# A hybrid attention and Fourier encoder layer: two operand splits issued later, and the middle frequency's column in one product with the first group's columns

## The chip, the cores and the metric

The kernel runs on one core of one Trainium2 chip. The metric is the device time of one execution in microseconds; the median of the runs counts. One execution was taken with the hardware profiler; its rows give start times in microseconds from the start of its span.

## The reference

One encoder layer is applied to a prompt of 256 tokens and, apart from it, to a sample of 2048 tokens, both 1024 wide, in float32.

```python
def encoder_layer(x, w_in, rpb, w_fourier, b_fourier, g_pre, g_na, g_f, w_out, g_post):
    h = rms_norm(x, g_pre)
    proj = h @ w_in
    q, k, v, z_a, u_f, z_f = jnp.split(proj, ...)
    y_a = neighbourhood_attention(q, k, v, rpb)
    y_f = fourier_mix(u_f, w_fourier, b_fourier)
    mixed = jnp.concatenate([rms_norm(y_a, g_na) * jax.nn.silu(z_a),
                             rms_norm(y_f, g_f) * jax.nn.silu(z_f)], axis=-1)
    out = mixed @ w_out
    return x + rms_norm(out, g_post)

def fourier_mix(u, w_f, b_f):
    ...
    spec = jnp.fft.fft2(ug, axes=(1, 3), norm='ortho')
    mixed = spec.real.reshape(b, s, F_WIDTH).astype(u.dtype)
    return mixed @ w_f + b_f
```

Six projections of 512 columns each leave the normed input. The attention looks at a window of 8 by 16 positions of a grid 64 wide. The Fourier part takes the real part of a transform over the tokens and over 64 columns of each of 8 groups.

## The kernel before, in words

**Precise products.** A float32 operand is split into a high half, a cast to a shorter form (ScalarE, ACT), and a low half, the remainder that the cast leaves (VectorE, DVE). A product is then three matmuls on TensorE (PE): high by high (L171), high by low (L172 or L173) and low by high. `mm3` issues them in this order. So each operand needs its cast, and then its remainder, ahead of the matmul that reads it. Products that are not split (the Fourier stage's `dft`, L1005) run in plain float32, and the trace shows each such product as two PE rows.

**The stages.** The trace has, in order: products for the prompt (weights folded with the norm's gains, the first tokens); 16 blocks of the prompt's other projections (`for b in range(16)`, PE rows `mm<-ph,wl` and the like, up to 121.5 us), whose weight blocks are split by `b_raw` (L577 cast `wh`, L578 remainder `wl`) two blocks ahead; the stage `vu(0)`, from 121.5 us on, which makes the sample's first half of the `v` and `u` projections; the sample's other projections; the Fourier stage (`stage2`, from 553 us on); attention and the output.

**vu(0) and its operands.** `vu` makes two outputs with seven products in place of eight: sums of blocks of the input times sums of blocks of the weights. There are 14 groups of 12 matmuls (seven products j = 0 to 6, two column strips s each, in the order 0 0 1 1 2 2 3 3 4 4 5 5 6 6). A group i at place j reads

- the operand `bnew[0, j]`, that is the high half `xh` and the remainder `xl` of a 128 by 2048 block of the sample, made by `n_first(j)`: the cast at L444 on ACT, the subtraction at L445 on DVE. Sums of such blocks come from `n_sum` (L439). `xl` is first read by the third matmul of its group (L173);
- the weight `op_[j]`, `vh` and `vl`, two halves each, made by `op_split` (L493 and L494, for j = 5 L489 and L490); `op_split(0)` and `op_split(1)` stand in blocks 14 and 15, the others in vu(0) at i = 2, 4, 6, 8 and 10. The weights from j = 2 on are loaded by `op_load` (L479) from a scratch tensor.

Each group's result leaves PSUM with a copy (L524 on ACT) or an addition (L521 on DVE: `uc`, `u`, `vuo`), and `vuo` is stored by SyncE (L364).

What else is done in vu(0) comes from a table of hooks, by the group index i: `n_first`, `rows_load` (L300, 1 MB of rows `xm`), `rows_square` (L305, two squares on ACT that add up a row's squares), `w_load`, `w_sums` (L548 on POOL, GpSimd) and `a_split` (L562, L563) of the next stage's weights. Row block x + 5 is loaded at i = 2x + 1 and squared at i = 2x + 4 for x = 0 to 3. The operands `xh`, `xl`, the blocks `nx` and the rows `xm` share one pool of 16 buffers of a megabyte each (tag `k8`).

Before the change `n_first` stands at block 3 (j = 0), 5 (j = 1), 12 (j = 2), 13 (j = 3) and in vu(0) at i = 0, 3 and 6 (j = 4, 5, 6). The engines work through their instructions in order. The order on each is close to the program's, but a tool places the instructions, so that it isn't word for word that of the code.

**stage2.** The Fourier transform over the tokens has two steps; `stage2(gq, zg, c)` is the second one, for four quarters gq and five column pieces c. For each pair it makes the 256 columns of a PSUM tile `pab` in four products of 64 columns (c = 4: four of three parts each), one per group g, with the matrices `d2`. `split_ab` then takes a high half (`split_ps`, L997; on DVE if gq = 0 and c < 3, else on ACT; L1012 for c = 4) and a remainder (L998, L1014) of them. For gq = 0 there is one more column, the middle frequency: a product of one column with `dnyq`, in a PSUM tile of its own, `pny` (tag `a`, three buffers), and its own `split_ab`. `pab` takes turns through three buffers: `b`, `b`, `c`, so that the fourth product reuses the first's, the fifth the second's and so on. Just before, DVE clears two PSUM tiles `ptb` (L975).

`dnyq` (128 by 4) holds the one-column matrix in column 0, zeros in 1 and a mask of partitions in column 2, which `pq` reads (L1055). It is loaded once, long before (L917).

Of the kernel before, what the change touches and what calls it, by code (L numbers as in the profile page):

```python
# [10 lines left out]
F32 = mybir.dt.float32  # L11
# [34 lines left out]
def constants():  # L46
    c = {}
    c["ident"] = np.eye(128, dtype=np.float32)
    n1 = np.arange(128)
    f1 = np.zeros((128, 128))  # L50
    for k1 in range(64):
        f1[:, 2 * k1] = np.cos(2 * np.pi * ((k1 * n1) % 128) / 128)
        f1[:, 2 * k1 + 1] = np.sin(2 * np.pi * ((k1 * n1) % 128) / 128) if k1 else (-1.0) ** n1
    c["f1"] = f1.reshape(32, 4, 128).transpose(1, 0, 2).reshape(128, 128)
    nrm = 1.0 / np.sqrt(2048 * 64)
    n2 = np.arange(16)
    d = np.zeros((128, 16, 128))
    for g in range(16):
        for kl in range(4):
            k1 = 4 * g + kl  # L60
            for k2 in range(16):
                if k1:
                    k = k1 + 128 * k2
                elif k2 < 8:
                    k = 128 * k2
                else:
                    k = 64 + 128 * (k2 - 8)
                co = np.cos(2 * np.pi * ((n2 * k) % 2048) / 2048) * nrm
                si = np.sin(2 * np.pi * ((n2 * k) % 2048) / 2048) * nrm
                ca = k2 * 4 + kl  # L70
                cb = 64 + ca
                r0 = (kl * 2) * 16 + n2
                r1 = (kl * 2 + 1) * 16 + n2
                if k1:
                    d[r0, g, ca] = co
                    d[r1, g, ca] = -si
                    d[r0, g, cb] = si
                    d[r1, g, cb] = co
                else:
                    r = r0 if k2 < 8 else r1  # L80
                    d[r, g, ca] = co
                    d[r, g, cb] = si
    c["d2"] = d
    dn = np.zeros((128, 4))
    dn[:16, 0] = ((-1.0) ** n2) * nrm
    dn[:, 2] = np.arange(128) % 32 != 0
    c["dnyq"] = dn
    n = np.arange(256)[:, None]
    k = np.arange(129)[None, :]
    ang = 2 * np.pi * ((n * k) % 256) / 256  # L90
    f256 = np.concatenate([np.cos(ang), np.sin(ang)], axis=1) / np.sqrt(256 * 64)
    c["f256"] = f256.reshape(4, 2, 32, 258).transpose(0, 2, 1, 3).reshape(128, 2, 258)
    f = np.arange(64)
    sl = np.arange(32)
    cs = np.zeros((128, 2, 64))
    for b in range(2):
        rows, cols = slice(64 * b, 64 * b + 64), slice(32 * b, 32 * b + 32)
        ang = 2 * np.pi * ((f[:, None] * sl[None, :]) % 64) / 64
        cs[rows, 0, cols] = np.cos(ang)
        cs[rows, 1, cols] = np.where(sl == 0, (-1.0) ** f[:, None], np.sin(ang))  # L100
    c["cs"] = cs
    cm = np.zeros((128, 2, 32))
    cs_ = np.zeros((128, 80))
    rm = np.zeros((128, 16))
    for p in range(128):
        half, i, qc = p // 64, p // 16 % 4, p % 16
        for b in range(2):
            cb = 2 * b + half
            ws = min(max(16 * cb + qc - 8, 0), 48)
            kc = KP0[cb] + np.arange(32)  # L110
            cm[p, b] = np.where((kc >= ws) & (kc < ws + 16), 0.0, BIG)
        for cb, j in ((0, slice(0, 24)), (1, slice(24, 56)), (3, slice(56, 80))):
            ws = min(max(16 * cb + qc - 8, 0), 48)
            kc = KC0[cb] + np.arange(KW[cb])
            cs_[p, j] = np.where((kc >= ws) & (kc < ws + 16), 0.0, BIG)
        j = np.array(ORD[half])
        rm[p, :11] = np.where((j >= i) & (j < i + 8), 0.0, BIG)
    c["cmask"] = cm.reshape(128, 64)
    c["csmask"] = cs_
    c["rmask"] = rm  # L120
    return {k: np.ascontiguousarray(v.astype(np.float32)) for k, v in c.items()}
# [54 lines left out]
def build(tc, A, O):  # L176
# [3 lines left out]
    cst = es.enter_context(tc.tile_pool(name="cst", bufs=1))  # L180
# [27 lines left out]
    invt = cst.tile([128, 18], F32, name="invt")  # L208
    invf = cst.tile([128, 18], F32, name="invf")
    inva = cst.tile([128, 18], F32, name="inva")  # L210
    dnyq = cst.tile([128, 4], F32, name="dnyq")
    cm = cst.tile([128, 80], F32, name="cm")[:, :64].rearrange("p (b x) -> p b x", b=2)


# [528 lines left out]
    for b in range(16):  # L743
        kind, blk = divmod(b, 4)
        if b < 10:
            wz_load(1)
        if b in (0, 2):
            n_load((b // 2, 1))
        if b == 10:
            op_load(0)  # L750
        if b == 12:
            op_load(1)
        if b < 14:
            b_raw(b + 2)
        if b < 8:
            x, y = divmod(b, 2)
            n_scale(None, *divmod(x, 2)[::-1], range(2 * y, 2 * y + 2))
        elif b < 12:
            n_sum(b - 8)
        if b in (3, 5, 12, 13):  # L760
            n_first((3, 5, 12, 13).index(b))
        if b > 13:
            op_split(b - 14)
        p = mmt(512)[:, :TP]
        wh, wl = wb.pop(b)
        for k in range(KC):
            mm3(nc, p, wh[:, k], wl[:, k], hp_[:, k], lp_[:, k], k == 0, k == KC - 1)
        o = st.tile([128, 256], F32, tag="f", name="f", bufs=3)
        if kind == 1:
            v = [(o, p)]  # L770
        elif kind == 3:
            v = [(o[:, 128 * x:128 * x + 128].rearrange("p (x r c) -> p r x c", x=2, c=16),
                  p[:, 128 * x:128 * x + 128].rearrange("p (r x c) -> p r x c", x=2, c=16)) for x in range(2)]
        else:
            v = [(o.rearrange("p (r b c) -> p b r c", b=2, c=32), p.rearrange("p (b r c) -> p b r c", b=2, c=32))]
        for d, i in v:
            nc.scalar.activation(d, i, AF.Silu if kind < 2 else AF.Copy, scale=-0.125 if kind == 3 else 1.0)
        if kind < 2:
            nc.sync.dma_start(zD[kind, blk * 128:blk * 128 + 128, :TP], o)
        else:  # L780
            nc.sync.dma_start((kD if kind == 2 else qD)[blk, :, :TP], o)
# [14 lines left out]
    def at(i, f, *a):  # L796
        hooks.setdefault(i, []).append(call(f, *a))

    for x in range(4, 7):
        at(3 * x - 12, n_first, x)  # L800
    for x in range(4):
        at(2 * x + 1, rows_load, x + 5)
        at(2 * x + 4, rows_square, x + 5)
# [212 lines left out]
    def stage2(gq, zg, c):  # L1016
        m = int(c in (2, 3))
        np_ = 96 if c == 4 else 128
        x = (gq * 5 + c) % 3 == 2
        p = ps.tile([np_, 4, 64], F32, tag="c" if x else "b", name="pab", bufs=1 if x else 2)  # L1020
        for g in range(4):
            dft(p[:, g, :], c, [(zg[g], d2[gq // 2][:, (gq % 2) * 4 + g, m * 64:m * 64 + 64])])
        split_ab(gq, c, lambda a: a[:, :1024].rearrange("p (k q g l) -> p q g k l", k=16, q=4, g=4)[:, gq],
                 p.rearrange("p g (k l) -> p g k l", l=4))
        if gq == 0:
            p = ps.tile([np_, 1], F32, tag="a", name="pny")
            dft(p, c, [(zg[0], dnyq[:, m:m + 1])])
            split_ab(gq, c, lambda a: a[:, 1024:1025], p)
        if gq == 2:
            p = ps.tile([np_, 129], F32, tag="a", name="pup")  # L1030
            dft(p, c, [(up[:, t], f256[:, t, 129 * m:129 * m + 129]) for t in range(2)])
            split_ab(gq, c, lambda a: a[:, 1025:1154], p)
# [6 lines left out]
    def pq(m):  # L1039
        PQ[m] = [gt([128, 2, 512], F32R, "pq" + x) for x in "hl"]  # L1040
        pp = [ps.tile([128, 512], F32, tag="a", name="ppq") for b in range(2)]
        for j in range(4):
            for b in range(2):
                rs = slice(64 * b, 64 * b + 64)
                nc.tensor.matmul(pp[b][32 * j:32 * j + 32], cs2[rs, m, 32 * b:32 * b + 32], wf[rs, j, :], start=True,
                                 stop=True)
        for b, p in enumerate(pp):
            h, l = PQ[m][0][:, b], PQ[m][1][:, b]
            if m == 0:
                split_ps(h, l, p)  # L1050
                continue
            t = sm.tile([128, 512], F32, name="wt%d" % b)
            nc.scalar.copy(t, p)
            nc.scalar.dma_start(wr32[16 * b:16 * b + 16:4], t[::32])
            keep = dnyq[:, 2:3]  # L1055
            nc.scalar.activation(h, p, AF.Copy, scale=keep)
            nc.vector.scalar_tensor_tensor(out=l, in0=p, scalar=keep, in1=h.bitcast(F32), op0=ALU.mult,
                                           op1=ALU.subtract)
# [514 lines left out]
    for k in range(2, len(G) + 2):  # L1573
# [17 lines left out]
        x = k // 2  # L1591
# [196 lines left out]
```

## Time and profile before

| what | value |
|---|---|
| runs | 937.64, 939.05, 938.73 us |
| median | 938.73 us |
| profiled execution | 937.48 us |
| its span, first to last instruction | 935.7 us |
| granted TensorE clock in it, mean | 0.999 |

So 1.8 us of the profiled execution lie around the span, and it was 1.25 us below the median. A timeline row reads: start, duration, engine, line, operation, output from inputs, sizes, count, and in brackets the idle time of the engine ahead of it with what ended that. Where a row stands for several instructions (x2), the duration is that of all. PE rows overlap: a matmul's duration is longer than the step to the next one. A row of the chain of waits reads: start, the time it holds, engine, output, line. A row of the windows reads: the stretch, its length, busy time of PE, PEld (weight loads), DVE, ACT and POOL with their counts, the granted clock, the share of the DMA engines and GB/s.

### The profile page before, as it was taken

What the parts mean: (1) busy time and instruction counts of PE and PEld (TensorE: products, weight loads), DVE (VectorE), ACT (ScalarE), POOL (GpSimd) and SP (SyncE); (2) the same over time, 40 slices, a digit from 0 to 9 for tenths busy, and PEclk for the clock granted to TensorE, in tenths of its full rate; (3) what the DMA queues carried; (4) which work ended last, traced back from release to release, by engine and by line L of the source; (5) the groups of instructions that cost most, each with busy time, mean ns of one, the idle gap of its engine ahead of it and who ended that gap; (6) DMA issues with size and microseconds to landing.
All of it is one profiled execution on the core that took longest, in us unless ns stands there. A gap on an engine that the chain in (4) does not pass through costs nothing.

```text
span 935.7 us, 18895 instructions
## 1 busy us (share of the span) xinstructions
PE 925.3 (99%) x6790; PEld 774.5 (83%) x6790; DVE 669.9 (72%) x1308; ACT 469.8 (50%) x1038; POOL 332.0 (35%) x337
## 2 busy tenths in 40 slices
PE   9999999999999999999999999999999999999997
PEld 7889988888888888888888888978788887888886
DVE  6487997688864967597666645677665666659997
ACT  5856577623332743233334425667655666654443
POOL 3200002436650300363333200445456565525444
PEclk9999999999999999999999999999999999999999
DMA  9899777468573999758888789888779899879993
GB/s 323 329 360 400 217 253 281 158 246 314 201 288 151 352 400 359 265 209 316 294 310 286 273 287 309 295 262 257 245 248 274 264 300 283 255 237 377 341 340 128
DMA packets 144829, 264.04 MB, mean 282 GB/s; under 512 B 21784, under 2 KB 84632, under 8 KB 141984
## 3 DMA queue, kind: packets, MB, share of 16 engines
q1 hardware_dynamic: 144576, 262.81, 80.9%
q8 instruction: 54, 0.88, 0.4%
q14 instruction: 39, 0.32, 0.1%
q10 hardware_dynamic: 160, 0.02, 0.0%
HBM read 174.75 MB, written 95.35 MB: 289 GB/s over the span
## 4 chain that ended last, share of the span: by engine, by line
PE 94%; DMA 3%; DVE 2%; issue 1%; ACT 0%; DVEq 0%; SPq 0%
PE mm L172 18%; PE mm L173 18%; PE mm L171 17%; PE ptb L1425 10%; PE po L1425 10%; PE pv L1508 5%; PE ptb L1485 3%; PE s L1179 3%; PE pab L1005 2%; PE ptb L1179 2%; DMA woD<-wo 1%; PE py L171 1%; PE py L173 1%; PE py L172 1%; PE pf L1425 1%
## 5 line engine op out<-in xcount | busy, mean ns | idle before, releaser
L171 PE MATMUL mm<-xh,wa 128*128 128x512 f32 x448 | 174.4, 389 | 0.0
L173 PE MATMUL mm<-xh,wa 128*128 128x512 f32 x448 | 174.3, 389 | 0.0
L172 PE MATMUL mm<-xl,wa 128*128 128x512 f32 x448 | 174.3, 389 | 0.0
L548 POOL TENSOR_TENSOR ws<-wr 128x512 f32<-128x512 f32 x16 | 22.2, 1386 | 259.3 <-DMA wr<-wz 246.2
L171 PEld LDWEIGHTS mm<-xh,wa 128*128 128x128 f32 x448 | 84.1, 188 | 17.5
L173 PEld LDWEIGHTS mm<-xh,wa 128*128 128x128 f32 x448 | 84.1, 188 | 17.4
L172 PEld LDWEIGHTS mm<-xl,wa 128*128 128x128 f32 x448 | 84.1, 188 | 17.4
L1425 PE MATMUL po<-w,yh 128*128 128x512 f32 x280 | 86.8, 391 | 0.0
L1425 PE MATMUL ptb<-wo,yh 128*128 128x512 f32 x272 | 86.7, 400 | 0.0
L1213 POOL TENSOR_SCALAR w<-w,m 128x352 f32<-128x352 f32 (+4 forms) x136 | 75.4, 572 | 30.4 <-PE s L1179 14.0
L563 DVE TENSOR_TENSOR wa<-wr,wa 128x512 fp32r<-128x512 f32 x60 | 57.7, 969 | 30.6 <-ACT wa L562 30.3
L1206 ACT ACTIVATE w<-w,m 128x352 f32<-128x352 f32 (+4 forms) x136 | 69.9, 521 | 12.5 <-DVE m L1201 12.1
L861 DVE TENSOR_TENSOR f<-u,mm 128x512 f32<-128x512 f32 x64 | 43.6, 681 | 34.1 <-PE mm L173 29.5
L172 PE MATMUL mm<-vl,xh 128*128 128x512 f32 x168 | 65.6, 390 | 0.4 <-DVE vl L494 0.4
L171 PE MATMUL mm<-vh,xh 128*128 128x512 f32 x168 | 65.4, 389 | 0.0
L173 PE MATMUL mm<-vh,xl 128*128 128x512 f32 x168 | 65.4, 389 | 0.0
L1425 PEld LDWEIGHTS ptb<-wo,yh 128*128 128x128 f32 x272 | 49.3, 188 | 14.8 <-ACT sqa L1536 3.4
L1425 PEld LDWEIGHTS po<-w,yh 128*128 128x128 f32 x280 | 52.3, 188 | 11.0
L562 ACT CAST wa<-wr 128x512 fp32r<-128x512 f32 x60 | 36.5, 617 | 42.7 <-PE mm L173 16.8
L1508 PEld LDWEIGHTS pv<-pt,v 96*64 96x64 f32 (+2 forms) x1280 | 45.2, 137 | 11.6 <-issue 6.6
L1425 PE MATMUL po<-w,yl 128*128 128x512 f32 x140 | 54.5, 389 | 0.0
L1425 PE MATMUL ptb<-wo,yl 128*128 128x512 f32 x136 | 53.1, 391 | 0.0
(249 smaller groups left out, 2192.3 us busy)
## 6 DMA issues: line engine op xcount, KB each, us to landing
wr<-wz SPq DMA_DIRECT2D x48, 512.0 KB
vl<-sD SPq DMA_DIRECT2D x20, 512.0 KB
xm<-xm SPq DMA_DIRECT2D x9, 1024.0 KB
oD<-ofs SPq DMA_DIRECT2D x18, 512.0 KB
of<-oD SPq DMA_DIRECT2D x18, 512.0 KB
yr<-yD SPq DMA_DIRECT2D x34, 256.0 KB
zD<-f SPq DMA_DIRECT2D x16, 512.0 KB
woD<-wo SPq DMA_DIRECT2D x16, 512.0 KB
```

The source lines that it names most:

```text
L171: nc.tensor.matmul(out, lh, rh, start=first, stop=False)
L172: nc.tensor.matmul(out, lh, rl, start=False, stop=False)
L173: nc.tensor.matmul(out, ll, rh, start=False, stop=last)
L562: nc.scalar.copy(o[:, 0], src)
L563: nc.vector.tensor_tensor(out=o[:, 1], in0=src, in1=o[:, 0].bitcast(F32), op=ALU.subtract)
L861: nc.vector.tensor_tensor(out=dst(f, b), in0=src(uu[u]), in1=src(p), op=op)
L1179: nc.tensor.matmul(sp[2 * b + h][64 * y:64 * y + 64, j * w:(j + n) * w], g["q"][hs, 128 * b + 64 * y:128 * b + 64 * y + 64], kk[hs, k:k + ...
L1206: nc.scalar.activation(w, w, AF.Exp, bias=m[:, h:h + 1], scale=-1.0, accum_out=m[:, 2 + h:3 + h])
L1213: nc.gpsimd.tensor_scalar(w, w, m[:, 4 + h:5 + h], 1.0, ALU.mult, ALU.mult)
L1425: nc.tensor.matmul(p, (d["l"] if x == 2 else d["h"])[:, c], w(n, int(x == 1), c), start=j == 0, stop=j == 11)
L1485: nc.tensor.transpose(ptb[2 * b + y][:nk, x:x + 64], g["w"][b][ys, h, c0:c0 + nk], ident[ys, ys])
L1508: nc.tensor.matmul(p[hs, b, o], v[:nk, b, x, hs], g["pt"][b][:nk, h, j * 128 + o.start:j * 128 + o.stop], start=first, stop=last)
```

## The change

It has two edits.

First, the splits of operands 2 to 6 of vu(0). `n_first(2)` moves from block 12 to block 13; `n_first(3)` from block 13 into vu(0) at i = 1; `n_first(4)`, `(5)` and `(6)` from i = 0, 3, 6 to i = 4, 7, 10.

Second, the middle frequency. `dnyq` grows to 128 by 2 by 66: for each of the two matrices m the 64 columns of the first group, then the middle frequency's column at 64 and the mask at 65. The tile `pab` grows from 256 to 260 columns. The groups are made from the last to the first, so that the first group's stands at the end, and for gq = 0 its product takes 65 columns from `dnyq`. The tile `pny` and its products go; `split_ab` of the single column reads column 256 of `pab`. The views are turned accordingly.

```diff
-    dn = np.zeros((128, 4))
-    dn[:16, 0] = ((-1.0) ** n2) * nrm
-    dn[:, 2] = np.arange(128) % 32 != 0
+    dn = np.zeros((128, 2, 66))
+    dn[:, :, :64] = d[:, 0].reshape(128, 2, 64)
+    dn[:16, 0, 64] = ((-1.0) ** n2) * nrm
+    dn[:, 0, 65] = np.arange(128) % 32 != 0
...
-    dnyq = cst.tile([128, 4], F32, name="dnyq")
+    dnyq = cst.tile([128, 2, 66], F32, name="dnyq")
...
-        if b in (3, 5, 12, 13):
-            n_first((3, 5, 12, 13).index(b))
+        if b in (3, 5, 13):
+            n_first((3, 5, 13).index(b))
...
-    for x in range(4, 7):
-        at(3 * x - 12, n_first, x)
+    for x in range(3, 7):
+        at(3 * x - 8 if x > 3 else 1, n_first, x)
...
-        p = ps.tile([np_, 4, 64], F32, tag="c" if x else "b", name="pab", bufs=1 if x else 2)
-        for g in range(4):
-            dft(p[:, g, :], c, [(zg[g], d2[gq // 2][:, (gq % 2) * 4 + g, m * 64:m * 64 + 64])])
-        split_ab(gq, c, lambda a: a[:, :1024].rearrange("p (k q g l) -> p q g k l", k=16, q=4, g=4)[:, gq],
-                 p.rearrange("p g (k l) -> p g k l", l=4))
+        p = ps.tile([np_, 260], F32, tag="c" if x else "b", name="pab", bufs=1 if x else 2)
+        for g in range(3, -1, -1):
+            s = 64 * (3 - g)
+            if gq == 0 and g == 0:
+                dft(p[:, s:s + 65], c, [(zg[g], dnyq[:, m, :65])])
+            else:
+                dft(p[:, s:s + 64], c, [(zg[g], d2[gq // 2][:, (gq % 2) * 4 + g, m * 64:m * 64 + 64])])
+        split_ab(gq, c, lambda a: a[:, :1024].rearrange("p (k q g l) -> p q g k l", k=16, q=4, g=4)[:, gq, ::-1],
+                 p[:, :256].rearrange("p (g k l) -> p g k l", g=4, l=4))
         if gq == 0:
-            p = ps.tile([np_, 1], F32, tag="a", name="pny")
-            dft(p, c, [(zg[0], dnyq[:, m:m + 1])])
-            split_ab(gq, c, lambda a: a[:, 1024:1025], p)
+            split_ab(gq, c, lambda a: a[:, 1024:1025], p[:, 256:257])
...
-            keep = dnyq[:, 2:3]
+            keep = dnyq[:, 0, 65:66]
```

## The prediction

> **What bounds the kernel now.** I read the page first: the engines' shares and the chain that ended last.
>
> ```profile
> PE 925.3 (99%) x6790; PEld 774.5 (83%) x6790; DVE 669.9 (72%) x1308; ACT 469.8 (50%) x1038; POOL 332.0 (35%) x337
> PE 94%; DMA 3%; DVE 2%; issue 1%; ACT 0%; DVEq 0%; SPq 0%
> ```
>
> TensorE (PE) is busy almost throughout and carries the chain, so time is won only by taking work from PE or by ending one of its waits, and a new PE wait costs its full length. Next, what PE waits for:
>
> ```profile
> PE mm L173 <- DVE wl L578: 0.8, 4, 0.2
> PE mm L172 <- DVE vl L494: 0.4, 2, 0.2
> ```
>
> These are VectorE (DVE) remainders at the seam between the prompt blocks and the stage vu(0), where the change works. PE's timeline there:
>
> ```profile
> 118.17 0.28 PE L171 MATMUL mm<-ph,wh 128*128 128x256 f32 x1
> 118.29 0.28 PE L172 MATMUL mm<-pl,wh 128*128 128x256 f32 x1
> 118.77 0.39 PE L173 MATMUL mm<-ph,wl 128*128 128x256 f32 x1 [0.20 <-DVE wl L578]
> 118.99 0.28 PE L171 MATMUL mm<-ph,wh 128*128 128x256 f32 x1
> ...
> 121.50 0.39 PE L171 MATMUL mm<-vh,xh 128*128 128x512 f32 x1
> 122.11 0.50 PE L172 MATMUL mm<-vl,xh 128*128 128x512 f32 x1 [0.21 <-DVE vl L494]
> ```
>
> Products follow each other every 0.12 us; before 118.77 the step is 0.48 and after it 0.22, so one wait costs 0.36 + 0.10 = 0.46 us. At 122.11 the step is 0.61 where 512-column products take 0.23, so 0.38 and about 0.10 to restart, 0.48. Elsewhere up to the middle-frequency products PE has no gap worth a term.
>
> **First edit: the splits of operands 2 to 6 go later.** I write F2 to F6 for them. Each has a ScalarE (ACT) cast and a DVE remainder. On DVE's chain at the seam:
>
> ```profile
> 115.38 0.64 DVE xl L445
> 117.47 0.79 DVE wl L578
> ```
>
> The xl is F2's remainder, and F3's comes right behind that wl: each pushes the wl or vl for which PE then waits. Now the last block's wl stands directly behind the wl before it, at about 115.3, then F2, then the vl at 115.3 + 1.1 + 2.2 = 118.6, ready at 119.8, where PE wants it at about 121.3. So the waits at 118.77 and 122.11 go and nothing is late in their place. Of the four waits for wl in the list, the earlier ones stay: they stand behind sums (L439) that aren't moved. Gain: 0.46 + 0.48 = **0.94 us**; the least is 0.46, if the vl should still be late.
>
> When PE wants F2 to F6: vu(0) begins at 121.50 - 0.46 = 121.0 and its 14 groups take 12 x 0.227 = 2.72 us each. F2 is used from the fifth group (131.9), F3 from the seventh (137.3), F4 from the ninth (142.8), F5 from the eleventh (148.2), F6 from the thirteenth (153.7). F2 is made by 118.6, F3 behind the four vl by 126; both have ten microseconds to spare, under PE's groups. F4 is split at the fifth group's place, behind two additions and two vl pairs, and has some four left. F5 and F6 are the ones in doubt.
>
> ACT's list in vu(0) around F5 and F6, before (L444 are the casts of F5 and F6, L305 the squares of row blocks 5 and 6):
>
> ```order
> L444 CAST xh<-nx 128x2048
> L493 CAST vh<-vl 128x1024 x2
> L305 ACTIVATE xm,ssq<-xm 128x1024 x2
> L493 CAST vh<-vl 128x1024 x2
> L444 CAST xh<-nx 128x2048
> L305 ACTIVATE xm,ssq<-xm 128x1024 x2
> L489 ACTIVATE vh<-vl 128x1024 x2
> ```
>
> And now (F4, squares 5, squares 6, F5, squares 7, F6; each line is one later in the changed file):
>
> ```order
> L445 CAST xh<-nt 128x2048
> L306 ACTIVATE xm,ssq<-xm 128x1024 x2
> L494 CAST vh<-vl 128x1024 x2
> L306 ACTIVATE xm,ssq<-xm 128x1024 x2
> L445 CAST xh<-nx 128x2048
> L490 ACTIVATE vh<-vl 128x1024 x2
> L306 ACTIVATE xm,ssq<-xm 128x1024 x2
> L494 CAST vh<-vl 128x1024 x2
> L445 CAST xh<-nx 128x2048
> ```
>
> F5 now stands behind the squares of block 6, F6 behind those of block 7, and the squares wait for loads. ACT and the SyncE queue in the trace:
>
> ```profile
> 139.11 1.05 ACT L493 CAST vh<-vl 128x1024 fp32r<-128x1024 f32 x1 [0.19 <-DMA vl<-sD]
> 140.06 1.91 ACT L444 CAST xh<-nx 128x2048 fp32r<-128x2048 f32 x1
> 141.88 1.05 ACT L305 ACTIVATE xm<-xm 128x1024 f32<-128x1024 f32 x1
> 147.40 1.06 ACT L305 ACTIVATE xm<-xm 128x1024 f32<-128x1024 f32 x1 [1.44 <-DMA xm<-xm]
> ```
>
> ```profile
> 133.60 0.38 SPq L300 DMA_DIRECT2D xm<-xm  x1
> 135.01 0.32 SPq L364 DMA_DIRECT2D vN<-vuo  x1
> 135.42 1.35 SPq L479 DMA_DIRECT2D vl<-sD  x2
> 136.87 0.44 SPq L300 DMA_DIRECT2D xm<-xm  x1
> ```
>
> ```profile
> 144.00:148.00 4.00, 4.00 (x19) 3.33 (x18) 3.90 (x4) 2.56 (x4) 0.00 (x0) 1.00 1.02 415
> ```
>
> The last row is the stretch from 144 to 148: DMA share 1.02 at 415 GB/s, so the queue is full. SyncE's and POOL's orders don't change. Between the landing at 139.11 and that of block 7 at 147.40 lie block 6 (1.05 MB), a store (0.26), two vl (1.05) and block 7 (1.05): 3.41 MB in 8.29 us, 411 GB/s. So block 6 lands near 139.11 + 2.55 = 141.7, or up to 0.9 sooner with the seam gone; I take 141.1. Squares 2.1 (two of 1.05), then F5's cast 1.91: F5's remainder starts near 145.1. In the trace before DVE did F6 at 144.10, and F5 long ahead. DVE's list before, from F5 to the pair of L490 (xl is an operand's remainder, vl a weight's, and L521 the additions that empty PE's groups):
>
> ```order
> L445 TENSOR_TENSOR xl<-nx,xh 128x2048
> L521 TENSOR_TENSOR vuo<-uc,mm 128x512
> L494 TENSOR_TENSOR vl<-vl,vh 128x1024 x2
> L521 TENSOR_TENSOR uc<-uc,mm 128x512 x2
> L494 TENSOR_TENSOR vl<-vl,vh 128x1024 x2
> L445 TENSOR_TENSOR xl<-nx,xh 128x2048
> L521 TENSOR_TENSOR u_1499<-uc,mm 128x512
> L521 TENSOR_TENSOR u_1516<-uc,mm 128x512
> L490 SCALAR_TENSOR_TENSOR vl<-vl,vh 128x1024 x2
> ```
>
> And now, from F5 to F6:
>
> ```order
> L446 TENSOR_TENSOR xl<-nx,xh 128x2048
> L522 TENSOR_TENSOR u_1512<-uc,mm 128x512
> L491 SCALAR_TENSOR_TENSOR vl<-vl,vh 128x1024 x2
> L522 TENSOR_TENSOR vuo<-u_1491,mm 128x512
> L522 TENSOR_TENSOR uc<-uc,mm 128x512
> L522 TENSOR_TENSOR vuo<-u_1512,mm 128x512
> L522 TENSOR_TENSOR uc<-uc,mm 128x512
> L495 TENSOR_TENSOR vl<-vl,vh 128x1024 x2
> L446 TENSOR_TENSOR xl<-nx,xh 128x2048
> ```
>
> F6 moved from the head of this run of work to its tail. The run's length is in the trace of before, where DVE goes through the same pieces without a gap:
>
> ```profile
> 144.10 2.29 DVE L445 TENSOR_TENSOR xl<-nx,xh 128x2048 fp32r<-128x2048 f32 x1 [2.60 <-ACT xm L305]
> 146.31 1.28 DVE L521 TENSOR_TENSOR u<-uc,mm 128x512 f32<-128x512 f32 x2
> 147.50 2.36 DVE L490 SCALAR_TENSOR_TENSOR vl<-vl,vh 128x1024 fp32r<-128x1024 f32 x2
> ...
> 152.16 2.36 DVE L494 TENSOR_TENSOR vl<-vl,vh 128x1024 fp32r<-128x1024 f32 x2
> ```
>
> From start to start: F5 2.21 (144.10 to 146.31), one addition 0.60 (half of the two), a vl pair and four additions 4.66 (147.50 to 152.16), another pair 2.27 (its 2.36 less the overlap with what follows), F6 2.29: 12.03 us. F6 is ready at 145.1 + 12.0 = 157.1. PE wants it at the third product of its thirteenth group:
>
> ```profile
> 155.11 0.39 PE L173 MATMUL mm<-vh,xl 128*128 128x512 f32 x1
> ```
>
> that is at 155.11 - 0.94 = 154.2. PE stands still about **3.0 us**. It partly shows already at the vl pair behind F5; that is the same delay, not another one. Bounds: with block 6 at 141.7 it is 3.6. If F5 came early, F6's cast would still follow block 7's squares (147.40 + 2.1), two casts (2.1) and its own 1.91, so the remainder ends near 155.8: 1.6 us at least with block 7 as late as before.
>
> **GpSimd beside F6.** POOL's first sum starts just then:
>
> ```profile
> 155.82 1.85 POOL L548 TENSOR_TENSOR ws<-wr 128x512 f32<-128x512 f32 x1 [126.92 <-DMA wr<-wz]
> 159.72 2.81 DVE L563 TENSOR_TENSOR wa<-ws,wa 128x512 fp32r<-128x512 f32 x2 [2.61 <-ACT wa L562]
> ```
>
> A pair that took 2.36/2 each for twice the size takes 2.81 here beside POOL. F6's remainder starts near 154.8, a microsecond ahead of POOL, so I charge nothing; if POOL comes first, up to 1.85. The Trainium skill, SBUF — State Buffer, "Who interferes with whom", says that a DVE instruction with two SBUF inputs and a GpSimd instruction that reads SBUF exclude each other for the whole instruction, whichever starts first; by it the price here is nothing or up to POOL's own length, and the 2.81 agrees with such a hold.
>
> **Second edit: the middle column joins the 64.** The five pny products go:
>
> ```profile
> 553.99 0.34 PE L1005 MATMUL pny<-dnyq,zg 128*128 128x1 f32 x2
> 554.18 1.08 PE L1005 MATMUL pab<-d,zg 128*128 128x64 f32 x8
> ...
> 556.42 1.08 PE L1005 MATMUL pab<-d,zg 128*128 128x64 f32 x8
> ...
> 558.16 0.24 PE L1005 MATMUL pny<-dnyq,zg 128*32 128x1 f32 x6
> 558.33 5.47 PE L1005 MATMUL pab<-d,zg 128*128 128x64 f32 x64
> ```
>
> Each holds PE for 0.17 (558.16 to 558.33) to 0.2 (553.99 to 554.18), **1.0 us** in five. One more column beside 64 is a sixty-fourth of a product that takes 0.2, nothing; the groups' reversed order and the mask's other column change no count and no size. But the single column now lives in pab's own PSUM buffer, which is free for the fourth product only when the first one's single-column remainder is done. DVE's list before, from the first remainder:
>
> ```order
> L998 TENSOR_TENSOR abl_4861<-pab,abh_4860 128x4x16x4
> L998 TENSOR_TENSOR abl_4861<-pny,abh_4860 128x1
> L997 CAST abh_4860<-pab 128x4x16x4
> L997 CAST abh_4860<-pny 128x1
> L997 CAST abh_4862<-pab 128x4x16x4
> ```
>
> Now:
>
> ```order
> L999 TENSOR_TENSOR abl_4861<-pab,abh_4860 128x4x16x4
> L998 CAST abh_4860<-pab 128x1
> L998 CAST abh_4860<-pab 128x4x16x4
> L999 TENSOR_TENSOR abl_4861<-pab,abh_4860 128x1
> L999 TENSOR_TENSOR abl_4861<-pab,abh_4860 128x4x16x4
> L998 CAST abh_4860<-pab 128x1
> L998 CAST abh_4862<-pab 128x4x16x4
> L999 TENSOR_TENSOR abl_4861<-pab,abh_4860 128x1
> L999 TENSOR_TENSOR abl_4863<-pab,abh_4862 128x4x16x4
> L998 CAST abh_4862<-pab 128x1
> L999 TENSOR_TENSOR abl_4863<-pab,abh_4862 128x4x16x4
> L999 TENSOR_TENSOR abl_4863<-pab,abh_4862 128x1
> ```
>
> Each single remainder moved behind the next product's large row, and the third one's (last row) behind the fourth's remainder. DVE is the busy one:
>
> ```profile
> 555.52 0.42 DVE L998 TENSOR_TENSOR abl<-pab,abh 128x256 fp32r<-128x256 f32 x1
> ...
> 557.99 0.42 DVE L998 TENSOR_TENSOR abl<-pab,abh 128x256 fp32r<-128x256 f32 x1 [0.35 <-ACT abh L997]
> ```
>
> First remainder 555.52, two casts 0.07 + 0.33 and the wait for the single one: it ends near 556.4, and the fourth product starts at 556.45, as before (wanted at 555.83, three pny sooner). The sixth waits for the row behind 557.99 + 0.42, about 558.55, against 558.33 before; the eighth once more for the fifth's single remainder, 0.2. So I expect +0.4 in place of -1.0, with bounds -1.0 and +0.9. The larger dnyq load (66 KB more at 411 GB/s is 0.16 us of DMA) lies far from either place and under PE's work.
>
> **Sum.** -0.94 + 3.0 + 0.4 = +2.5 us. The profiled execution took 937.48, 1.25 below the median; the sum is on the difference, so 938.73 + 2.5 = **941.2**. A measurement tells about 0.2% (1.9 us) from no change.
>
> **Rivals.** (a) F5 and F6 are in time after all, so it is not slower: block 6's rows would have to be there by about 138.2, 3 us sooner, so that DVE's run ends by 154.2. For it speaks only the seam's 0.9; against it the queue, 411 GB/s with no room. Time -0.94 + 0.4: 938.2; with the pny gain kept, -1.94: 936.8. Chance 0.10, of which the last 0.04. (b) DVE's run is not what ends last but F6's own cast: wait 1.6, sum +1.1, 939.8; 0.17. (c) The single column's remainder frees the PSUM buffer by 555.8 (DVE would have to be done 0.6 sooner at the first product), so that the gain of 1.0 holds beside the wait in vu(0): -0.94 + 3.0 - 1.0 = +1.1, 939.8; 0.08. (d) POOL comes ahead of F6: +1.8 more, 943.0; 0.07. The forecast itself: 0.58, +1.7 to +3.4, 940.4 to 942.1.
>
> **Numbers.** Range 938.6 to 942.9: (a) mostly out, (d) in. Faster by over 0.2%: 0.06, from (a) with the pny gain. Within: (b), (c), the rest of (a) and the low end of the forecast, 0.36. Slower: 0.58.
>
> **What would show it.** Right: no PE wait at the last wl and the first vl; a PE wait on xl (L446) of about 2 to 3 us in vu(0), with F5's cast behind block 6's squares; pab starts 0.1 to 0.4 later at the sixth to ninth product. Wrong: F6's remainder done before PE's thirteenth group, or the ninth product starting a microsecond sooner relative to the first.

## The result and the profile after

The changed kernel is slower than forecast, and its times are scattered. Four executions took 943.8, 943.97, 957.45 and 961.99 us, median 950.71; the kernel before had a median of 938.45 us beside them (937.64 to 939.05). The ratio is 1.0103, 95% interval 1.0054 to 1.0153. That ratio leaves out the execution of 961.99 us as disturbed; what follows shows that the scatter is the kernel's own, so the single times are given throughout. Six executions more (e10 below) took 943.18 to 956.89, median 953.52. The forecast was 941.2, at most 942.9.

The profiled execution is the one of 961.99 us. TensorE's (PE's) waits in it, as total, times and longest in us:

```profile
PE mm L174 <- DVE xl L446: 3.1, 1, 3.1
PE mm L173 <- DVE vl L491: 1.6, 1, 1.6
PE mm L174 <- DVE wl L579: 1.3, 3, 0.8
PE pab L1006 <- DVE abl L999: 0.6, 1, 0.6
```

The waits that were forecast are there: for F6's remainder, for the vl pair behind F5, and ahead of the fourth `pab`. But they add up to 5.3 us, and the execution is 24.5 us longer. Three PE rows divide the time. Of the kernel before (a wait for wl near the end of the prompt blocks, the first product of stage2, the first product behind it):

```profile
115.43 0.39 PE L173 MATMUL mm<-ph,wl 128*128 128x256 f32 x1 [0.21 <-DVE wl L578]
...
553.15 1.00 PE L1005 MATMUL pab<-d,zg 128*128 128x64 f32 x8
...
576.44 0.45 PE L171 MATMUL py<-abh,pqh 128*128 128x386 f32 x1
```

And of the changed kernel:

```profile
118.00 0.39 PE L174 MATMUL mm<-ph,wl 128*128 128x256 f32 x1 [0.20 <-DVE wl L579]
...
561.38 0.78 PE L1006 MATMUL pab<-d,zg 128*128 128x64 f32 x6
...
599.59 0.69 PE L172 MATMUL py<-abh,pqh 128*128 128x386 f32 x1
```

From the first to the second row it is 437.72 us before and 443.38 after, 5.7 more: the seam and vu(0). From the second to the third it is 23.29 and 38.21, 14.9 more: stage2. The 2.6 us ahead of the first row belong to what comes before the changed places; the same row stands at 114.97 us in e1 and at 117.35 in e2, so executions differ there by as much. The 1.4 us that are left come behind the third row.

Windows of the changed kernel across stage2 (after the length come the busy times of PE, PEld, DVE, ACT and POOL, then the granted clock, the DMA share and GB/s):

```profile
560.00:564.00 4.00, 4.00 (x31) 3.74 (x29) 2.22 (x5) 2.38 (x3) 0.52 (x1) 1.00 0.32 131
564.00:568.00 4.00, 3.28 (x39) 2.88 (x39) 3.02 (x14) 1.46 (x4) 0.00 (x0) 0.75 0.96 303
568.00:572.00 4.00, 4.00 (x21) 4.00 (x21) 1.00 (x3) 0.80 (x3) 0.00 (x0) 0.50 1.07 396
...
596.00:600.00 4.00, 4.00 (x41) 3.04 (x34) 1.71 (x3) 1.73 (x5) 0.00 (x0) 0.50 0.79 267
...
604.00:608.00 4.00, 4.00 (x25) 4.00 (x24) 2.43 (x10) 2.08 (x4) 0.00 (x0) 1.00 0.32 111
```

The clock is 1.0 up to about 566 us, then 0.50 for some 37 us, through the rest of stage2, and full again behind 603. PE is "busy" all the time at half speed: no list of waits shows this loss. The kernel before has 1.00 throughout (552 to 580 us), in two of its windows:

```profile
556.00:560.00 4.00, 4.00 (x61) 3.97 (x61) 2.79 (x14) 1.66 (x6) 0.00 (x0) 1.00 1.00 311
564.00:568.00 4.00, 4.00 (x38) 4.00 (x38) 2.07 (x6) 1.90 (x7) 0.00 (x0) 1.00 1.00 406
```

What stands at the edge in the changed kernel:

```profile
563.78 0.39 PE L1006 MATMUL pab<-dnyq,zg 128*128 128x65 f32 x2
564.78 0.85 PE L1006 MATMUL pab<-d,zg 128*128 128x64 f32 x6 [0.61 <-DVE abl L999]
```

The fourth `pab` waits 0.61 us for the first one's single remainder. Within two microseconds the clock is down.

The mean clock of each execution divides the four in the same way: 0.976 and 0.977 in the two long ones, 0.996 in those of 943.8 and 943.97 us. So these two lost little or no clock in stage2, and still took 5.4 us more than the kernel before, about what the first edit alone costs in e1 below.

In vu(0), ACT shows the order that was forecast, squares (L306) of a loaded block ahead of F5's cast (L445), and DVE the run of work from F5 to F6:

```profile
144.77 1.06 ACT L306 ACTIVATE xm<-xm 128x1024 f32<-128x1024 f32 x1 [1.41 <-DMA xm<-xm]
...
146.87 1.89 ACT L445 CAST xh<-nx 128x2048 fp32r<-128x2048 f32 x1
```

```profile
148.79 2.29 DVE L446 TENSOR_TENSOR xl<-nx,xh 128x2048 fp32r<-128x2048 f32 x1 [3.58 <-ACT xh L445]
...
158.53 3.36 DVE L446 TENSOR_TENSOR xl<-nx,xh 128x2048 fp32r<-128x2048 f32 x1
```

```profile
158.34 1.40 POOL L549 TENSOR_TENSOR ws<-wr 128x512 f32<-128x512 f32 x1 [128.58 <-PE mm L173]
```

F6's remainder takes 3.36 us in place of 2.29: POOL's sum began 0.2 us ahead of it (in e8 below, the remainder began 1.85 us ahead of POOL, and took 2.29). Here, too, the clock fell, once PE had stood still:

```profile
164.00:166.00 2.00, 2.00 (x6) 1.52 (x6) 2.00 (x3) 1.36 (x3) 1.32 (x2) 0.50 0.05 13
166.00:168.00 2.00, 2.00 (x9) 1.60 (x8) 2.00 (x3) 0.07 (x1) 0.69 (x1) 0.85 0.34 131
```

but only for about 3.4 us, among products of 512 columns, which costs 1.7 us. The account of the first stretch closes: -0.94 at the seam, 1.65 + 3.11 of waits with 0.1 each to restart, and 1.7, is 5.7.

### The profile page after: what moved, and what is told of

The parts are those of the page before. It is cut to its first block, busy times and chain, and to the rows that moved or that the text cites. A ratio compares the mean times of both kernels' runs of the same rounds, so it can differ in the third digit from the quotient of the medians.

```text
span 960.2 us, 18865 instructions
## 1 busy us (share of the span) xinstructions
PE 944.6 (98%) x6776; PEld 790.3 (82%) x6776; DVE 671.0 (70%) x1308; ACT 470.3 (49%) x1038; POOL 332.8 (35%) x337
## 4 chain that ended last, share of the span: by engine, by line
PE 93%; DMA 3%; DVE 2%; issue 1%; ACT 0%; SPq 0%; DVEq 0%
PE mm L174 17%; PE mm L173 17%; PE mm L172 17%; PE ptb L1428 10%; PE po L1428 10%; PE pv L1511 5%; PE pab L1006 3%; PE ptb L1488 3%; PE s L1182 2%; PE ptb L1182 2%; PE py L172 1%; DMA wr<-wz 1%; PE py L173 1%; PE py L174 1%; DMA xm<-xm 1%
## 5 line engine op out<-in xcount | busy, mean ns | idle before, releaser
L564 DVE TENSOR_TENSOR wa<-wr,wa 128x512 fp32r<-128x512 f32 x60 | 59.7, 1002 | 35.0 <-ACT wa L563 35.0
```

Source lines behind the costliest of these rows:

```text
L564: nc.vector.tensor_tensor(out=o[:, 1], in0=src, in1=o[:, 0].bitcast(F32), op=ALU.subtract)
```

## The experiments

The theory after the result: PE's waits do cost what they last, but some of them also bring the granted clock down to a half; among dense products it comes back in about 3.4 us, among stage2's small ones it stays down for tens of microseconds. Rivals: the long executions come from the chip or from vu(0); the product of 65 columns or the shared tile is itself dear; the clock, once fallen, is held for a fixed time.

**e1: the first edit alone.** `stage2` and `dnyq` as before; `n_first` as in the change.

> The first edit alone; stage2 as before. Theory (waits of TensorE, and a granted clock that falls after some of them): the two waits in vu(0), 1.6 and 3.1 us in the trace of the changed kernel, are there again, with a fall of the clock to a half for about 3.4 us behind them, 1.7 us. With 0.9 us won at the seam the time is 943 to 944 us, and no execution takes 955 or more, since stage2 has no new wait. Rival (the long executions come from the chip or from vu(0)): some executions here take 955 us or more too.

Six executions: 940.61 to 945.87 us, median 943.76, beside 938.76 of the kernel before; ratio 1.0054, interval 1.0034 to 1.0073. None is at 950. The waits are there, in its profile 1.1 and 3.1 us, and the time from the wait for wl to the first `pab` (114.97 to 556.12 us) is 441.15, 3.4 more than before. In that execution the clock did not fall behind the 3.1 us:

```profile
158.00:160.00 2.00, 1.63 (x7) 1.37 (x8) 2.00 (x4) 0.50 (x1) 2.00 (x2) 1.00 0.14 49
```

So a wait of the same length took the clock down in one execution and not in another, unlike what was expected; the part behind e10 gives a reading of what set the two apart. The scatter from 940.6 to 945.9 is no wider than that of the kernel before beside it (936.65 to 942.04). The long executions do not come from vu(0).

**e2: the second edit alone.** `dnyq` and `stage2` as in the change; `n_first` as before.

> The second edit alone; the operands are split where they were before. Theory: TensorE waits some 0.6 us for the single column's remainder ahead of the fourth product in stage2, and then in some executions, not in all, the granted clock falls to a half and stays there for 35 to 40 us, through all of the small products: about 938.5 us in some, 953 to 957 us in others. Rival 1 (the long executions come from the chip or from vu(0)): all executions within 1 us of the kernel before. Rival 2 (the product of 65 columns is itself dear): every execution slower by the same amount.

Twelve executions: 937.76 and 938.93 us, and ten from 947.1 to 955.77; median 950.25. The kernel before had 936.65 to 942.04 in 29 executions. Its profile has one new wait, the same 0.61 us, and behind it:

```profile
556.00:560.00 4.00, 3.39 (x41) 3.19 (x41) 3.50 (x14) 2.64 (x3) 0.00 (x0) 0.93 0.64 225
560.00:564.00 4.00, 3.94 (x34) 3.73 (x28) 1.65 (x6) 0.93 (x5) 0.00 (x0) 0.50 1.03 358
...
596.00:600.00 4.00, 4.00 (x21) 4.00 (x21) 1.40 (x8) 1.17 (x2) 0.00 (x0) 0.87 0.47 147
```

Two heaps, as the theory had it: not every execution loses its clock. The mean clock agrees: 0.997 and 0.998 in the two short executions, 0.977 to 0.988 in the ten long ones. The upper heap is wider than expected; five of the ten lie below 953 us. That two of twelve are as fast as before speaks against a product that is itself dear.

**e3: the second edit without its wait.** As e2, but

```diff
-        x = (gq * 5 + c) % 3 == 2
-        p = ps.tile([np_, 260], F32, tag="c" if x else "b", name="pab", bufs=1 if x else 2)
+        x = gq * 5 + c
+        x = "bbcaaa"[x] if x < 6 else "bbc"[x % 3]
+        p = ps.tile([np_, 260], F32, tag=x, name="pab", bufs={"a": 3, "b": 2, "c": 1}[x])
```

> The second edit alone, with the first six pab tiles in six different PSUM buffers (tags b, b, c, a, a, a), so that none of them waits for a single column's remainder. Theory: no wait in stage2, no fall of the clock, 1.0 us of one-column products gone: 937 to 938 us in every execution. Rival 1 (it isn't the wait that lowers the clock): some executions of 953 us and more here too. Rival 2 (the product of 65 columns is itself dear): slower than the kernel before.

Twelve executions: 936.74 to 939.33 us, median 937.76; ratio 0.9988, interval 0.9976 to 1.0. No long one. The same products, the same 65 columns, and no wait:

```profile
575.42 0.44 PE L172 MATMUL py<-abh,pqh 128*128 128x386 f32 x1
...
578.54 0.42 PE L1262 MATMUL py<-a,w 96*128 96x386 f32 x1 [0.58 <-DVE w L1066]
```

Its first `pab` starts at 553.05, so stage2 takes 22.37 us, 0.92 less than before: the one-column products are worth what was forecast. The last row shows 0.58 of it given back at a product that waits for `w32`, which is made from rows that come by a DMA. From the first `pab` to that product it is 25.49 us, 25.74 before.

**e4: only the moves of operands 2 and 3.** The kernel before, with `n_first(2)` in block 13 and

```diff
-    for x in range(4, 7):
-        at(3 * x - 12, n_first, x)
+    for x in range(3, 7):
+        at(3 * x - 12 if x > 3 else 1, n_first, x)
```

> Of the first edit only the moves of operands 2 and 3; operands 4 to 6 are split at i = 0, 3 and 6 as before, and stage2 is as before. Theory: the two waits at the seam go (0.9 us), nothing is late in vu(0): 937.5 to 938 us. Rival (the third operand's split in vu(0) pushes the later ones as much): a wait in vu(0) of a microsecond or more, 939 us and above.

Twelve executions: 937.0 to 939.94 us, median 937.56; ratio 0.9992, interval 0.998 to 1.0004: no difference that can be told. In its trace the gain is there:

```profile
116.22 0.38 PE L173 MATMUL mm<-ph,wl 128*128 128x256 f32 x1 [0.21 <-DVE wl L578]
...
552.99 1.00 PE L1005 MATMUL pab<-d,zg 128*128 128x64 f32 x8
```

436.77 us against 437.72 before, 0.95 less; the forecast was 0.94.

**e5: dense work behind the wait.** As e2, and behind the first quarter's last product, for `gq == 0 and c == 4`:

```diff
+                hot = ps.tile([128, 512], F32, tag="a", name="dense")
+                for i in range(10):
+                    nc.tensor.matmul(hot, zgs[0][0][:, :128], zgs[0][0], start=True, stop=True)
```

> The second edit alone, with its wait, and behind the first quarter's last product ten more products of 512 columns, float32, whose result nobody reads: about 4.5 us of dense work at full clock that the kernel does not need. Theory (small products don't lift a clock that has fallen, dense ones do): the clock falls after the wait as before, is back at 1.0 some 4 us behind the start of the dense products, and stays there through the small products that follow. So no execution takes much longer than 938.5 + 4.5 + 4 = 947 us, although work was added to a kernel whose executions went up to 955.8. Rival (once fallen, the clock stays down for 35 to 40 us whatever runs): executions up to 960 us.

Four executions: 945.86 to 948.0 us, median 946.73. PE and the windows:

```profile
557.31 0.92 PE L1006 MATMUL pab<-d,zg 128*128 128x64 f32 x6 [0.61 <-DVE abl L999]
...
559.61 9.71 PE L1074 MATMUL dense<-zg 128*128 128x512 f32 x20
```

```profile
558.00:560.00 2.00, 2.00 (x29) 1.71 (x29) 0.97 (x5) 0.64 (x2) 0.00 (x0) 0.50 0.98 294
560.00:562.00 2.00, 2.00 (x4) 0.77 (x4) 0.74 (x3) 0.32 (x3) 0.00 (x0) 0.66 0.99 349
562.00:568.00 6.00, 6.00 (x16) 2.65 (x15) 0.00 (x0) 0.00 (x0) 0.00 (x0) 1.00 1.04 414
568.00:576.00 8.00, 8.00 (x83) 7.15 (x82) 2.81 (x7) 2.58 (x8) 1.27 (x1) 1.00 0.87 278
```

The same wait, the same fall; about 2 us into the dense products the clock is back, and it stays through the small ones that follow. The dense block held PE some 9.6 us (559.61 to 569.16), where 4.5 had been expected: ten products are twenty rows of nearly 0.5 us each, twice what had been taken; so two of the four executions are over the 947 expected. The kernel with 9.6 us of useless work is 3.5 us faster in the median than e2 without it (the kernel before had 938.68 us beside e5 and 938.76 beside e2). A hold of one fixed length is out.

**e6: a wait, but no edit.** The kernel before, with the fourth `pab` in the third one's buffer:

```diff
-        x = (gq * 5 + c) % 3 == 2
+        x = (gq * 5 + c) % 3 == 2 or gq * 5 + c == 3
```

> The kernel before, with neither edit, but the fourth pab tile put into the third one's PSUM buffer, so that its product waits for the third remainder, about 1.2 us. The operations are those of the kernel before. Theory (a wait of TensorE among the small products is what lowers the clock): most executions at 950 to 956 us. Rival (it takes the product of 65 columns or the shared tile): 939 to 940.5 us, the wait alone.

Four executions: 949.16 to 955.15 us, median 950.64.

```profile
557.57 1.94 PE L1005 MATMUL pab<-d,zg 128*128 128x64 f32 x8 [1.17 <-DVE abh L997]
```

```profile
558.00:560.00 2.00, 2.00 (x19) 1.99 (x21) 0.01 (x1) 0.41 (x2) 0.00 (x0) 0.50 1.01 344
...
580.00:582.00 2.00, 2.00 (x33) 1.60 (x28) 0.79 (x3) 0.63 (x2) 0.00 (x0) 0.66 0.00 0
```

With the operations of the kernel before, a wait of 1.17 us costs 12 us in the median. Neither the 65 columns nor the shared tile is needed: the wait does it.

**e7: both edits without their waits.** e3 and e4 together.

> Both edits without their waits: operands 2 and 3 late, operands 4 to 6 at i = 0, 3, 6 as before, the middle column in the product of 65 columns, and six different PSUM buffers for the first six pab tiles. Theory: the gains add up, 0.9 and 1.0 us less: 936.5 to 937.2 us, no execution above 941. Rival (what is won is given back at a later wait): 937.5 us and above.

Eleven executions: 937.23 to 939.62 us, median 938.24 beside 938.68; ratio 0.9997, interval 0.9988 to 1.0007. No long execution, but the expected 936.5 to 937.2 was missed. Its trace has 0.9 us of wait for L491's vl pair in vu(0), where e4's had 0.2, so the first gain was nearly spent in that execution; the second one stands (553.84 to 576.23 us, 22.39). It is no better than the kernel before by what can be told, as the rival had it.

**e8 and e9: where operands 5 and 6 stand.** The first edit alone, with `n_first(5)` at i = 5 (e8), and with `n_first(5)` and `(6)` at i = 5 and 7 (e9). The line of e8, against the first edit's:

```diff
-        at(3 * x - 8 if x > 3 else 1, n_first, x)
+        at((1, 4, 5, 10)[x - 3], n_first, x)
```

> The first edit alone, but operand 5 is split at i = 5 in place of 7, so that its cast stands ahead of the squares of row block 6, which wait for a load; operand 6 still stands behind those of block 7. Theory (the casts are held behind squares that wait for loads): the wait for L490's remainder, 1.1 us, goes, and the wait for the sixth remainder shrinks from 3.1 to about 1.8 us, since its cast alone is now what is late: 940 to 941.5 us. Rival (GpSimd's sums hold VectorE, and the order of casts doesn't matter): no shorter than the first edit alone, 943 to 944 us.

Ten executions: 938.35 to 942.32 us, median 939.62, ratio 1.0017, interval 1.0005 to 1.0029; 4.1 us less than e1. One wait is left in vu(0):

```profile
156.81 0.50 PE L173 MATMUL mm<-vh,xl 128*128 128x512 f32 x1 [1.59 <-DVE xl L445]
```

1.6 us for F6 where 1.8 was expected, and none for the vl pair: F5's place behind block 6's squares was what started the run late.

> The first edit alone, with operands 5 and 6 split at i = 5 and 7 in place of 7 and 10, so that both casts stand ahead of the squares of the next row block; operands 2, 3 and 4 as late as in the change. Theory (lateness costs nothing as such, only standing behind squares that wait for loads does): no wait for a remainder of an operand in vu(0), 937.5 to 938.5 us. Rival (VectorE's work in vu(0) is too dense for late splits): a wait of a microsecond or more for the sixth remainder, 939.5 us and above.

Ten executions: 937.85 to 940.92 us, median 939.46, ratio 1.0005, interval 0.9995 to 1.0015. The expectation was missed: F6 is in time, but

```profile
151.27 0.50 PE L172 MATMUL mm<-vl,xh 128*128 128x512 f32 x1 [1.87 <-DVE vl L490]
```

Split at i = 7, F6 stands ahead of block 7's squares but still behind block 6's, which waited for their load until 143.16 us, and the fifth weight's halves now stand behind F6. In both runs it is what stands behind the squares that is late.

**e10: the change once more.**

> The changed kernel as it is, once more, for the spread of its times. Theory (the clock falls after the wait in stage2 in most executions, not in all): between 941 and 962 us, in two heaps, the lower at 941 to 945 and the upper at 950 to 962, with more in the upper. Rival (the first four executions were unlucky): nearly all at 941 to 945 us.

Six executions: 943.18, 946.78, 953.07, 953.97, 954.32 and 956.89 us, median 953.52; ratio 1.012, interval 1.0083 to 1.0157. Most are in the upper heap (mean clock 0.983 to 0.985); one lies between the two (0.995). In its profile the clock falls near 565 us and is back near 588, some 14 us sooner than in the first one:

```profile
566.00:568.00 2.00, 1.94 (x30) 1.60 (x29) 0.79 (x3) 0.80 (x3) 0.00 (x0) 0.50 1.03 327
...
588.00:590.00 2.00, 2.00 (x24) 1.33 (x24) 0.56 (x2) 0.54 (x2) 0.00 (x0) 0.83 0.00 0
```

So when it comes back differs, too, and with it the price.

**What the traces show together: steps of 3.41 us.** Windows with these borders hold the clock at a half from end to end (vu(0) and stage2 of the change, then stage2 of e10):

```profile
163.19:166.61 3.42, 3.42 (x9) 2.64 (x8) 3.42 (x4) 2.17 (x4) 2.74 (x2) 0.50 0.20 77
565.96:603.51 37.55, 37.44 (x264) 32.46 (x262) 12.33 (x30) 12.29 (x32) 1.27 (x1) 0.50 0.65 225
564.78:588.68 23.90, 23.84 (x177) 22.60 (x176) 7.85 (x25) 5.89 (x19) 1.25 (x1) 0.50 0.82 285
```

That is 1, 11 and 7 times 3.413 us. The other falls have the same lengths: 3.41 in e5 and in vu(0) of e10, 23.89 in e6, 37.54 in e2; and the full clock between the two falls of the change (166.61 to 565.96) lasts 117 times 3.413. So in these traces the clock changes only where one step of 3.41 us ends and the next begins. The steps that hold the long wait of vu(0), of e1 (counted back from the clock's change at 934.82, at the end of that trace) and of the change:

```profile
153.17:156.58 3.41, 2.10 (x10) 1.41 (x8) 3.41 (x3) 2.81 (x6) 1.66 (x2) 1.00 0.47 183
156.58:159.99 3.41, 1.62 (x7) 1.36 (x8) 3.41 (x4) 0.49 (x1) 3.41 (x2) 1.00 0.08 27
...
156.37:159.78 3.41, 2.47 (x11) 1.69 (x10) 3.41 (x3) 3.19 (x7) 1.40 (x1) 1.00 0.38 147
159.78:163.19 3.41, 1.24 (x5) 1.05 (x6) 3.41 (x3) 0.11 (x1) 3.37 (x2) 1.00 0.02 5
```

In e1 the wait lay across a border: PE was busy for 2.10 and 1.62 us of the two steps, and the clock stayed. In the change 1.24 us were left in one step, and the clock fell at its end. So, as these profiles read, the price of a wait also hangs on where it falls among the steps, and that differs between executions of one kernel: from the last wait for wl to the step border at which the clock fell in vu(0) it is 45.19 us in the change's first profile (118.00 to 163.19) and 44.05 in e10's (117.96 to 162.01). No run set this. That a wait of 0.61 us can be parted in the same way would account for the executions of e2 that lost nothing; no profile caught one.

## Why the prediction was wrong, point by point

- **The seam, -0.94:** right; 0.95 in e4, and no wait at the last wl nor the first vl in the changed kernel.
- **vu(0), +3.0:** the mechanism was right, the size was not. The run from F5 to F6 is 9.74 us from start to start (148.79 to 158.53), as added up. Two terms were too small. Block 6's squares began 1.1 us later than taken, seen from the same wait for wl: 144.77 - 2.57 = 142.2, where 141.1 was taken and 141.7 was the bound. SyncE issued its load when it had before (136.06 - 2.57 = 133.5, against 133.60): the seam's gain didn't bring it forward, and the landing had been worked out half a microsecond too early besides. And F6's remainder was held 1.07 us by POOL; that was rival (d) with a chance of 0.07. In e1, too, POOL began ahead of F6 (154.84 and 154.96 us). F6 was to begin a microsecond ahead of POOL and began 1.1 us later than forecast, POOL when it had before. With this PE's two waits are 4.4 to 5.0 us with their restarts.
- **stage2, +0.4:** the wait was placed rightly and is 0.61 us long; its own cost is about what was said (the fourth product starts 3.40 us behind the first one, 3.27 before). The rest of the +0.4, at the sixth and eighth product, can't be read here, since the clock had fallen by then.
- **The step that failed** is the first one, "a new PE wait costs its full length". It took the granted clock of 0.999 as given. It is not: behind a wait of 0.61 us stage2 took 14.9 us more in the profiled executions of the change and of e2 (555.13 to 593.35 us, 38.22), because PE ran at half clock for 37.5 us; the sum had +0.4 for all of stage2. Of the twelve executions of e2 ten paid 8 to 17 us, two nothing. No rival had the clock in it. The second miss is the size of the +3.0 for vu(0): the first edit alone, with no new wait in stage2, has a median of 943.76 us in e1, and the two executions of the change that kept the clock there took 943.8 and 943.97, all above the forecast's 942.9. The prediction was right that the kernel gets slower and by which waits, and wrong by the price of them.

The Trainium skill, TensorE: Matmul & The Clock Gate, Part 1, has the two states, half and full clock, that these windows show, and lets the clock fall after an idle window of about 3.4 us; by that rule neither the 0.61 us nor the 1.17 us would have lowered it, and here the measurement decides: they did. The Trainium skill, on the same page under "A second HAM failure mode", tells of small idle times between groups of matmuls that make the clock swing; that is nearer, only that here it does not swing but stays down for 23.9 or 37.5 us.

What stays open: which measure of PE's work the clock follows. It is not PE's busy time alone: the step of stage2 ahead of the fall was busy for 2.80 us in the change, more than the steps that kept the clock in e1. The runs show that small products keep a full clock that is never interrupted (before, e3: 1.00 through stage2), that products of 64 columns don't lift it once it has fallen (the change, e2, e6), and that dense ones do (e5); why a few executions of e2 went through the wait with nothing lost was not shown in a profile. In e6 and e10 the clock came back behind the products of 129 columns (`pup`) in stage2's third quarter, in e2 and the first profile of the change it did not. The step that ended with the rise held 16 rows of `pup` in e6 and 14 in e10, while in e2 and the change no step held more than 12; whether that decides it was not tried.

## What to carry to other kernels

Read the granted clock by stage, not only its mean: where TensorE runs small products, a wait of half a microsecond can cost ten and more, in some executions and not in others, and the list of waits doesn't show it, since the engine counts as busy. So a change that frees a buffer a little later is dear in such a stage, and a buffer more is worth having there even if it saves little. And of a step that is moved, look at what it comes to stand behind: here squares that wait for a load made everything behind them late, on two engines.

## What the runs showed of the hardware that was not expected

- In the profiled executions, a granted clock of 0.50 for 23.9 or 37.5 us behind TensorE waits of 0.61 and 1.17 us among products of 64 columns; 0 such falls in 12 executions of e3 with the same products and no wait, going by their times and mean clocks (0.996 to 0.999).
- All these stretches, and the 3.41 us in vu(0) and e5, are whole multiples of 3.413 us; a wait of 3.1 us across a border of these steps left the clock at 1.00 (e1).
- The fall does not come in every execution: e2 took 937.76 us in one and 955.77 in another.
- Twenty dense float32 passes of 512 columns, 9.6 us of work that nobody needs, made e2 3.5 us faster in the median.
- A DVE subtraction with two SBUF inputs took 3.36 us in place of 2.29 when a POOL sum had started 0.2 us ahead of it.
